# Layer 1: q and k turned by DMA, attention one group behind its pair group

## The chip, the cores and the metric

The kernel runs on one core of one Trainium2 chip. The metric is the device time of one execution in microseconds (us). The core has TensorE (matrix multiply, results to PSUM, eight banks of 128 partitions by 2 KB), VectorE, ScalarE, GpSimd, and SyncE, which issues most of the transfers; 16 DMA engines move the data.

## The reference

A decoder trunk of two layers over 256 tokens of width 2048, float32. Every layer is: RMSNorm, mixer, residual add, RMSNorm, SwiGLU FFN (hidden 5632), residual add; a last RMSNorm ends it. Layer 0 mixes with sliding-window attention beside an mLSTM. Layer 1, where the change lies, mixes with a forgetting attention of 16 heads of width 128:

```python
proj = xn @ w_in                         # (256, 2048) @ (2048, 3*2048 + 16)
q, k, v, f = split_cols(proj, FOX_SIZES)
log_f = jax.nn.log_sigmoid(f + b_f)
c = cumsum(log_f, axis=1)                # one bias per head and token
s = einsum('bhqd,bhkd->bhqk', q, k) * 128 ** -0.5
s = s + c[query] - c[key]                # causal: other scores are -inf
out = einsum('bhqk,bhkd->bhqd', softmax(s), v) @ w_out
```

## The kernel before

**Products.** Float32 operands are split into a high and a low part, and a product is three matmuls: high by high, high by low, low by high. A weight chunk is 256 rows by up to 512 columns (512 KB). `load_raw` (L111) loads it from SyncE's queue, `split_chunk` (L160) casts the high part on ScalarE (L163) and subtracts on VectorE (L164); six split chunks and four raw ones can be in flight. `gemm` (L177) is a plain product of one 512-column block, 12 matmuls of 512 columns per chunk (2 slices of k, 2 blocks of 128 tokens, 3 products).

**Pair groups.** `pair_group` (L487) makes two 512-column blocks at once, here q and k of four heads. It walks eight pairs of k slices in the order `QK_ORDER`; five are plain (24 matmuls), three are "mixed": a Strassen-like form of 21 matmuls, for which VectorE and ScalarE form sums and differences of the two weight chunks (L518 to L530) and split them. The second chunk of a mixed pair goes to a raw tile of the mixer's own pool (`od`, tag `raw`, two buffers). The plain sums take four PSUM banks of one pool and the products four of the other; `par` says which (`par` 0: plain sums in `pa`, products in `pm`). At the end the products are gathered in `c`, a tile of four 512-column rows (q of two token blocks, then k), and `fold` (L687) adds the plain sums, scaled by the norm.

**The mixer of layer 1** (from L1038) does this four times, for four heads each: a pair group; the values of the next group (`v_part`, a plain product in two `pm` banks), in parts that serve as filler; 16 turns of 128 by 128 blocks of q and k on TensorE (`transpose_many`, L297, matmuls with the identity at L301, evicted by VectorE at L302); and `attention` (L304). The last group's filler is the first part of the output product (`begin`), since no values are left.

**Attention** of four heads: scores in two halves (heads 0 and 2, then 1 and 3; L312, L319), scaled and biased on VectorE into `s` (L313, L320), which overlies `c`; maxima (L326); exponentials on ScalarE (L341); normalising on VectorE (L354). After a first `yield`, the probabilities are turned on TensorE (L363, L367). After a second, they meet the values (L371, L372), and the result is split into `mh` and `ml` (L382), the operand of the output product.

**Order.** The program is written once in Python; a scheduler with a timing model then fixes the order of each engine's queue. A higher place in the text means a higher priority; an instruction written later can be put ahead where the model finds it ready and the earlier one not. `tc.issue_after(x)` keeps what is written under it behind instruction `x`. On the chip, each queue runs in that order. `turn_scaled` (L251) and the FFN (L595 to L605) already turn tiles by DMA: a float32 tile is split into two planes of 16-bit halves (ScalarE), each plane is turned by one DMA transpose from SyncE's queue (`turn_planes`, L237), and the turned planes are joined again (ScalarE, L247 for the FFN).

Of the kernel before, what the change touches and what calls it, by code (L numbers as in the profile page):

```python
# [17 lines left out]
P = 128  # L18
# [6 lines left out]
CK = 2  # L25
# [35 lines left out]
def trunk(  # L61
# [90 lines left out]
        nc.sync.dma_start(bias_f, fox_b_f[0].partition_broadcast(P))  # L152

    latest = [None]

    def load_chunk(w, k0, c0, n):
        raw = ahead.pop(0) if ahead else load_raw(w, k0, c0, n)
# [19 lines left out]
    def gemm(acc, lhs, w, c0, n, k_from, k_to, k_all, skew=1):  # L177
        k0 = k_from
        while k0 < k_to:
            last = k_to == k_all and k0 + skew * CK >= k_all  # L180
            chunks = [load_chunk(w, kc, c0, n) for kc in range(k0, k_all if last else k0 + CK, CK)]
            order = [(i, t) for i in range(len(chunks) * CK) for t in range(NT)]
            if last:
                order.sort(key=lambda it: it[1])
            for i, t in order:
                k = k0 + i
                hi, lo = (c[:, i % CK, 0:n] for c in chunks[i // CK])
                ah, al = lhs(k)
# [4 lines left out]
                nc.tensor.matmul(o, al[:, ts], hi, start=False, stop=(k == k_all - 1))  # L193
            k0 += len(chunks) * CK

    def x_of(k):
# [104 lines left out]
            nc.tensor.transpose(pt[:, i, :], s_, ident)  # L301
        nc.vector.tensor_copy(dst, pt[:, 0:m, :])  # L302

    def attention(sp, q_of, k_of, v_of, dv, scale, bias0, bias1, k_tile, sinks=None, negc=None, s=None, ps=(pm, "pm")):  # L304
        if s is None:
            s = sp.tile([P, 4, 3 * P], F32, tag="s", name="s", bufs=2)
        for half in range(2):
            hs = slice(half, 4, 2)
            p0 = ps[0].tile([P, 2, P], F32, tag=ps[1], name="p0")
            for jj in range(2):  # L310
                j = 2 * jj + half
                nc.tensor.matmul(p0[:, jj, :], q_of(j, 0), k_of(j)[:, 0:P], start=True, stop=True)  # L312
            nc.vector.scalar_tensor_tensor(  # L313
                out=s[:, hs, 0:P], in0=p0, scalar=scale, in1=bias0[:, hs, :], op0=ALU.mult, op1=ALU.add
            )
            p1 = ps[0].tile([P, 2, S], F32, tag=ps[1], name="p1")
            for jj in range(2):
                j = 2 * jj + half
                nc.tensor.matmul(p1[:, jj, :], q_of(j, 1), k_of(j), start=True, stop=True)  # L319
            nc.vector.scalar_tensor_tensor(  # L320
                out=s[:, hs, P : 3 * P], in0=p1, scalar=scale, in1=bias1[:, hs, :], op0=ALU.mult, op1=ALU.add
            )
        parts = (slice(0, P), slice(P, 3 * P))
        mx = sm.tile([P, NT, 4], F32, tag="mx", name="mx")
        for b in range(NT):
            nc.vector.reduce_max(mx[:, b, :], s[:, :, parts[b]], axis=AX)  # L326
        neg = sm.tile([P, NT, 4], F32, tag="neg", name="neg")
        den = sm.tile([P, NT, 4], F32, tag="den", name="den")
        if sinks is not None:
# [7 lines left out]
            )  # L337
        for b in range(NT):
            for j in range(4):
                e = s[:, j, parts[b]]  # L340
                nc.scalar.activation(  # L341
                    e, e, AF.Exp, bias=neg[:, b, j : j + 1], accum_out=den[:, b, j : j + 1]
                )
        if sinks is not None:
# [5 lines left out]
        nc.vector.reciprocal(rec, den)  # L350
        for b in range(NT):
            for j in range(4):
                e = s[:, j, parts[b]]
# [4 lines left out]
        for half in range(2):  # L358
            pt = pm.tile([P, 2, S], F32, tag="pm", name="pp")
            for jj in range(2):  # L360
                j = 2 * half + jj
                for b in range(NT):
                    nc.tensor.transpose(pt[:, jj, b * P : (b + 1) * P], s[:, j, b * P : (b + 1) * P], ident)  # L363
            nc.scalar.copy(t0[:, 2 * half : 2 * half + 2, :], pt)
        pt = pm.tile([P, 4, P], F32, tag="pm", name="pp1")
        for j in range(4):
            nc.tensor.transpose(pt[:, j, :], s[:, j, 2 * P : 3 * P], ident)  # L367
        nc.vector.tensor_copy(t1, pt)

        def pv(po, j):  # L370
# [668 lines left out]
    with tc.tile_pool(name="od", bufs=1) as od:  # L1039
        def nat1(acc, n, name, bufs=1):  # L1040
            t_ = od.tile([P, NT, n], F32, tag=name, name=name, bufs=bufs)
            for t in range(NT):
                nc.scalar.mul(t_[:, t, :], acc[t][:, 0:n], r1[:, t : t + 1])
            return t_

        gemm(vacc0, x_of, wi1, c_v, NB, 12, KT, KT)
        vns = {0: nat1(vacc0, NB, "vn", bufs=2)}
        acc = tacc1
        gemm(acc, x_of, wi1, c_v + 14 * FD, VT + FOX_H, 8, KT, KT)
        fg = od.tile([P, NT, FOX_H], F32, name="fg")  # L1050
# [23 lines left out]
            j = mixed.index(pair)  # L1074
            return sx[0][:, j, :, :], sx[1][:, j, :, :]

        def v_part(i):
            vw = NB if i < 3 else VT
            acc = [bank(1, "vacc") for _ in range(NT)]

            def part(k0, k1):
                gemm(acc, x_of, wi1, c_v + i * NB, vw, k0, k1, KT)
                if k1 == KT:
                    vns[i] = nat1(acc, vw, "vn", bufs=2)

            return part
# [15 lines left out]
        for i in range(4):  # L1102
            qt = od.tile([P, 4, S], F32, tag="qt", name="qtf")
            kt = od.tile([P, 4, S], F32, tag="kt", name="ktf")
# [7 lines left out]
            if i == 3:  # L1112
                halves[:] = [halves[1], None]
            plain, c = pair_group(
                room, 0, x_of, sums_q, [(wi1, i * NB), (wi1, FOX_H * FD + i * NB)], QK_ORDER
            )
            fold(plain, c, (r1, r1))
            if i < 3:
                part = v_part(i + 1)
                fillers = [lambda k=k: part(k, k + 4) for k in (0, 4)] + [lambda: part(8, KT), lambda: None]  # L1120
            else:
                begun = [new_acc() for _ in range(2)]

                def begin(m, k0, k1):
                    return lambda: gemm(begun[m], m_of, w_out_odd[0], m * NB, NB, k0, k1, KT)

                def both(*some):
                    return lambda: [one() for one in some]

                fillers = [begin(0, 0, 4), begin(0, 4, 8), both(begin(0, 8, 12), begin(1, 0, 4)), begin(1, 4, 12)]  # L1130
            ps = (pa, "acc") if i < 3 else (pm, "pm")
            fillers.pop(0)()
            for m, dst in enumerate((qt, kt)):
                for g in range(0, 4, 2):
                    transpose_many(
                        dst[:, g : g + 2, :].rearrange("p g (t q) -> p (g t) q", q=P),
                        [c[:, 2 * m + t, (g + u) * FD : (g + u + 1) * FD] for u in range(2) for t in range(NT)],
                        ps,
                    )
            vn = vns[i]  # L1140

            def v_of(j, b, i=i, vn=vn):
# [4 lines left out]
            fillers.pop(0)()  # L1147
            for _ in attention(
                od,
                lambda j, b, qt=qt: qt[:, j, b * P : (b + 1) * P],  # L1150
                lambda j, kt=kt: kt[:, j, :],
                v_of,
                FD,
                FD**-0.5,
                cb0,
                cb1,
                4 * i,
                negc=negc[:, :, 4 * i : 4 * i + 4],
                s=c[:, :, 0 : 3 * P],
                ps=ps,  # L1160
            ):
                fillers.pop(0)()


    ov = out[0].rearrange("(t p) d -> p t d", p=P)
    fs = cp.tile([P, NT, 4], F32, name="fs")
# [27 lines left out]
    close_layer(1, w_out_odd[0], 3, "f1", begun=begun, finish=finish)  # L1194


_INS = [
# [46 lines left out]
```

## Time and profile before

| what | value |
|---|---|
| time, three runs | 2100.2, 2102.77, 2104.49 us; median 2102.77 |
| profiled execution | 2100.61 us, of which the span from first to last instruction is 2098.9 |
| TensorE busy | 2085.3 us, 99% of the span |
| VectorE, ScalarE busy | 1818.7 us (87%), 1325.4 us (63%) |
| DMA | 429.33 MB, mean 205 GB/s |
| mean granted TensorE clock | 0.999 |

A row of the stretches has its start and end, its length, then for each engine the busy time and the number of instructions, then the granted clock, the busy share of the DMA engines and GB/s. A row of a group has line, engine, operation, output and inputs, shapes and count; then the busy total, the mean ns of one; then the idle time of the engine before them and what ended it. A row of the chain has start, duration, engine, output, line and count. A row of the order in time has start, duration and the instruction, and in brackets the idle time before it. A row of the waits has who waited for whom, the total, the times and the longest. DMA issues have size and median us to landing.

### The profile page before, as it was taken

The page shows a single profiled execution, that of the slowest core. Times are in us where ns is not written, and L with a number is a line of the kernel's source. Part 1 is how long each engine was busy: PE and PEld are TensorE (multiplying, and loading weights), DVE is VectorE, ACT ScalarE, POOL GpSimd, SP SyncE. Part 2 cuts the span into 40 slices and gives each one's busy share as a digit, 9 for nine tenths or more (in the row PEclk, how much of TensorE's full clock was granted, in tenths as well). Part 3 has the DMA queues.
Part 4 walks back from the last instruction along what each step waited for, and adds up shares of the span by engine and source line. Part 5 has one row for each costly group of instructions (what it writes and reads, how often), then busy time and mean ns, then how long its engine had stood idle before and what let it go on. Part 6 is the DMA issues. An engine that isn't in the chain of part 4 may idle for free.

```text
span 2098.9 us, 26844 instructions
## 1 busy us (share of the span) xinstructions
PE 2085.3 (99%) x9582; PEld 1732.6 (83%) x9582; DVE 1818.7 (87%) x2402; ACT 1325.4 (63%) x1685; POOL 45.6 (2%) x70
## 2 busy tenths in 40 slices
PE   9999999999999999999999999999999999999998
PEld 7878888888888888888888888888888888888886
DVE  6689768998999999998898877679989999999985
ACT  7565568665577656667865555586755677556763
POOL 2100000000000000000000000000000000000000
PEclk9999999999999999999999999999999999999999
DMA  9446667766576657766775565577756676657763
GB/s 330 123 131 211 209 192 234 238 197 201 189 235 213 218 192 220 211 211 187 202 258 164 176 189 164 180 231 222 239 170 225 206 215 216 214 191 230 215 197 136
DMA packets 283318, 429.33 MB, mean 205 GB/s; under 512 B 80928, under 2 KB 89136, under 8 KB 283184
## 3 DMA queue, kind: packets, MB, share of 16 engines
q1 hardware_dynamic: 281424, 421.80, 64.8%
q0 software_dynamic: 1616, 5.78, 0.8%
q8 instruction: 75, 1.23, 0.2%
q14 instruction: 59, 0.48, 0.1%
q10 hardware_dynamic: 144, 0.03, 0.0%
HBM read 408.67 MB, written 2.11 MB: 196 GB/s over the span
## 4 chain that ended last, share of the span: by engine, by line
PE 92%; DVE 5%; issue 1%; DMA 1%; ACT 1%; POOLq 0%; POOL 0%; SPq 0%; DVEq 0%; ACTq 0%
PE acc L413 19%; PE acc L412 19%; PE acc L414 19%; PE acc L193 5%; PE acc L192 5%; PE acc L191 5%; PE prod L412 5%; PE prod L414 5%; PE prod L413 5%; DVE lo L164 2%; PE vacc L193 1%; PE vacc L192 1%; PE vacc L191 1%; DMA raw<-in_w_up_dram 1%; PE ptm L301 1%
## 5 line engine op out<-in xcount | busy, mean ns | idle before, releaser
L163 ACT CAST hi<-raw 128x1024 fp32r<-128x1024 f32 (+1 forms) x664 | 675.2, 1031 | 462.1 <-PE acc L414 223.3
L164 DVE TENSOR_TENSOR lo<-raw,hi 128x1024 fp32r<-128x1024 f32 (+1 forms) x664 | 785.8, 1198 | 137.0 <-ACT hi L163 135.0
L413 PE MATMUL acc<-lo,xh 128*128 128x512 f32 x1207 | 470.8, 390 | 0.4 <-DVE lo L164 0.4
L414 PE MATMUL acc<-hi,xl 128*128 128x512 f32 x1207 | 468.0, 390 | 0.0
L412 PE MATMUL acc<-hi,xh 128*128 128x512 f32 x1207 | 465.2, 390 | 1.0 <-DVE c L545 1.0
L412 PEld LDWEIGHTS acc<-hi,xh 128*128 128x128 f32 x1207 | 226.6, 188 | 49.1 <-DVE c L545 1.8
L413 PEld LDWEIGHTS acc<-lo,xh 128*128 128x128 f32 x1207 | 226.7, 188 | 47.5 <-DVE lo L164 0.7
L414 PEld LDWEIGHTS acc<-hi,xl 128*128 128x128 f32 x1207 | 226.7, 188 | 47.0
L413 PE MATMUL acc<-lo,mh 128*128 128x512 f32 x444 | 173.0, 390 | 0.0
L414 PE MATMUL acc<-hi,ml 128*128 128x512 f32 x444 | 171.5, 390 | 0.0
L412 PE MATMUL acc<-hi,mh 128*128 128x512 f32 x444 | 169.9, 390 | 0.0
L289 ACT CAST ht<-t 128x1024 fp32r<-128x1024 f32 x94 | 98.8, 1051 | 55.2 <-PE prod L414 48.7
L289 ACT CAST ht<-raw 128x1024 fp32r<-128x1024 f32 x94 | 98.6, 1049 | 44.6 <-PE acc L414 18.0
L191 PE MATMUL acc<-hi,mh 128*128 128x512 f32 x320 | 126.3, 396 | 0.0
L192 PE MATMUL acc<-lo,mh 128*128 128x512 f32 x320 | 125.0, 391 | 0.0
L193 PE MATMUL acc<-hi,ml 128*128 128x512 f32 x320 | 125.0, 393 | 0.0
L290 DVE TENSOR_TENSOR lt<-raw,ht 128x1024 fp32r<-128x1024 f32 x94 | 114.8, 1221 | 11.7 <-ACT ht L289 11.6
L289 ACT CAST hi<-raw 128x512 fp32r<-128x512 f32 (+1 forms) x115 | 72.3, 629 | 77.6 <-PE acc L414 60.8
L290 DVE TENSOR_TENSOR lt<-t,ht 128x1024 fp32r<-128x1024 f32 x94 | 114.6, 1219 | 5.5 <-ACT ht L289 5.5
L413 PEld LDWEIGHTS acc<-lo,mh 128*128 128x128 f32 x444 | 83.4, 188 | 17.3
L412 PEld LDWEIGHTS acc<-hi,mh 128*128 128x128 f32 x444 | 83.4, 188 | 17.3
L414 PEld LDWEIGHTS acc<-hi,ml 128*128 128x128 f32 x444 | 83.4, 188 | 17.1
(384 smaller groups left out, 3550.1 us busy)
## 6 DMA issues: line engine op xcount, KB each, us to landing
raw<-in_w_gate_dram SPq DMA_DIRECT2D x176, 512.0 KB, 4.6
raw<-in_w_up_dram SPq DMA_DIRECT2D x176, 512.0 KB, 4.7
raw<-in_w_down_dram SPq DMA_DIRECT2D x176, 512.0 KB, 4.8
raw<-in_w_in_odd_dram SPq DMA_DIRECT2D x88, 512.0 KB, 4.5
raw<-in_w_in_even_dram SPq DMA_DIRECT2D x64, 512.0 KB, 4.7
raw<-in_w_out_even_dram SPq DMA_DIRECT2D x32, 512.0 KB, 4.1
raw<-in_w_out_odd_dram SPq DMA_DIRECT2D x32, 512.0 KB, 4.9
raw<-in_w_in_odd_dram SPq DMA_DIRECT2D x8, 272.0 KB, 3.2
```

The costliest lines, as they stand in the source:

```text
L163: latest[0] = nc.scalar.copy(hi[:, :, 0:n], raw[:, :, 0:n])
L164: nc.vector.tensor_tensor(out=lo[:, :, 0:n], in0=raw[:, :, 0:n], in1=hi[:, :, 0:n].bitcast(F32), op=ALU.subtract)
L191: nc.tensor.matmul(o, ah[:, ts], hi, start=(k == 0), stop=False)
L192: nc.tensor.matmul(o, ah[:, ts], lo, start=False, stop=False)
L193: nc.tensor.matmul(o, al[:, ts], hi, start=False, stop=(k == k_all - 1))
L289: nc.scalar.copy(dst_h, src)
L290: nc.vector.tensor_tensor(out=dst_l, in0=src, in1=dst_h.bitcast(F32), op=ALU.subtract)
L301: nc.tensor.transpose(pt[:, i, :], s_, ident)
L412: nc.tensor.matmul(o, ah, hi, start=start, stop=False)
L413: nc.tensor.matmul(o, ah, lo, start=False, stop=False)
L414: nc.tensor.matmul(o, al, hi, start=False, stop=stop)
```

## The change

Pair groups of layer 1 run one ahead of the attention. Group 0 is only made; then, for i = 1 to 3, pair group i is made and group i-1 attended during the value product of group i; group 3 is attended at the end, with output products as filler. q and k of every group are turned by DMA, in the planes described above, in places that stand free at that time: the planes of q turn in `t0` or `t4`, those of k in small temporaries, and the heads go to `qt` and `kt` with two buffers each. The scores of groups 0 to 2 lie in the pool's two raw tiles, one per half, in place of `c`; for that `attention` takes `s` as two tiles, and its maxima are taken per half (four reduces in place of two) wherever it is called, layer 0 too. The first half's scores take `pa` banks, the second's `pm`. The values have one buffer and lie in `pa` banks; pair groups 1 to 3 have `par` 1. The special case of the last pair group's operand tiles (`halves[:] = [halves[1], None]`) goes.

```diff
+TURN_QK = (0, 1, 2, 3)
+SCORES_AT = -1
...
-    def attention(sp, ..., s=None, ps=(pm, "pm")):
+    def attention(sp, ..., s=None, ps=((pm, "pm"), (pm, "pm"))):
         if s is None:
-            s = sp.tile([P, 4, 3 * P], F32, tag="s", name="s", bufs=2)
+            whole = sp.tile([P, 4, 3 * P], F32, tag="s", name="s", bufs=2)
+            s = [whole[:, a:4:2, :] for a in range(2)]
...
         for b in range(NT):
-            nc.vector.reduce_max(mx[:, b, :], s[:, :, parts[b]], axis=AX)
+            for half in range(2):
+                nc.vector.reduce_max(mx[:, b, half:4:2], s[half][:, :, parts[b]], axis=AX)
...
-        vns = {0: nat1(vacc0, NB, "vn", bufs=2)}
+        vns = {0: nat1(vacc0, NB, "vn")}
...
+        def turn_heads(c, places):
+            cu = c.bitcast(U16).rearrange("p a (n b) -> p a n b", b=2)
+            heads, starts, joins = [], [], []
+            for m, turned in enumerate(places):
+                a = od.tile([P, 4, S], F32, tag=("qt", "kt")[m], name="heads", bufs=2)
+                au = a.rearrange("p g s -> p (g s)").bitcast(U16)
+                flat = au.rearrange("p (b n) -> p b n", b=2)
+                for b in range(2):
+                    nc.scalar.copy(flat[:, b, :].rearrange("p (t n) -> p t n", t=NT), cu[:, 2 * m : 2 * m + 2, :, b])
+                def start(flat=flat, turned=turned):
+                    with tc.issue_after(load[0].ins):
+                        turn_planes(turned, flat)
+                def join(au=au, turned=turned):
+                    cb = au.rearrange("p (n b) -> p n b", b=2)
+                    for b in range(2):
+                        nc.scalar.copy(
+                            cb[:, :, b].rearrange("p (g t q) -> p g t q", g=4, t=NT),
+                            turned[b].rearrange("p (t g) q -> p g t q", t=NT),
+                        )
...
+            return heads, starts + joins
...
         for i in range(4):
-            ... (pair group i with par 0, fold, values of i + 1 as filler,
-                 transpose_many of q and k, attention of i with s=c[:, :, 0 : 3 * P])
+            plain, c = pair_group(
+                room, min(i, 1), x_of, sums_q, [(wi1, i * NB), (wi1, FOX_H * FD + i * NB)], QK_ORDER, todo
+            )
+            fold(plain, c, (r1, r1))
+            if i == 0:
+                t0 = od.tile([P, 4, S], F32, tag="t0", name="turn0", bufs=1)
+                heads, steps = turn_heads(c, [place(t0.rearrange("p g s -> p (g s)")), small_places()])
+                todo = list(zip(TURN_QK, steps))
+                continue
+            t4 = room.t4()
+            new, steps = turn_heads(c, [place(t4.rearrange("p a n -> p (a n)")), small_places()])
+            spare = [od.tile([P, CK, NB], F32, tag="raw", name="s", bufs=2) ... for _ in range(2)]
+            gen = attend(i - 1, heads, spare, ((pa, "acc"), (pm, "pm")))
+            heads = new
+            w = NB if i < 3 else VT
+            vacc = [bank(0, "vacc") for _ in range(NT)]
+            if i == 3:
+                parts = [lambda a=a: values(a, a + 4) for a in range(0, 16, 4)]
+                parts += [lambda a=a: begin(0, a, a + 2) for a in range(0, 8, 2)]
+            else:
+                parts = [lambda a=a: values(a, a + 2) for a in range(0, 16, 2)]
+            for n, part in enumerate(parts):
+                if i == 3 and n == 4:
+                    begun[0] = new_acc()
+                if n == 0 and SCORES_AT < 0:
+                    next(gen)
+                part()
+                if n in (SCORES_AT, 4, 6):
+                    next(gen, None)
+                if n in (2, 3):
+                    run_next(steps)
+            vns[i] = nat1(vacc, w, "vn")
+            todo = list(enumerate(steps))
+        while steps:
+            with tc.issue_after(last_exp[0].ins):
+                run_next(steps)
+        begun[1] = new_acc()
+        gen = attend(3, heads, [c[:, a:4:2, 0 : 3 * P] for a in range(2)], ((pm, "pm"), (pm, "pm")))
+        begin(0, 8, 10)
+        with tc.issue_after(last_mm[0].ins):
+            next(gen)
+        begin(0, 10, 12)
+        begin(1, 0, 6)
+        next(gen)
+        begin(1, 6, 10)
+        next(gen, None)
+        begin(1, 10, 12)
```

`todo` hands steps to the next pair group: each is run at the named position of its walk, behind the cast of that position's chunk. `attend(i, ...)` is the former call of `attention` for group i, with the loads of its bias (`cb1`, `cb0`) ahead of it.

More of the change, by code (lines that the diff above doesn't have):

```diff
@@ L154, in trunk @@
     latest = [None]
+    last_mm = [None]
+    last_exp = [None]
     def load_chunk(w, k0, c0, n):
@@ L320, in attention @@
             nc.vector.scalar_tensor_tensor(
-                out=s[:, hs, P : 3 * P], in0=p1, scalar=scale, in1=bias1[:, hs, :], op0=ALU.mult, op1=ALU.add
+                out=s[half][:, :, P : 3 * P], in0=p1, scalar=scale, in1=bias1[:, hs, :], op0=ALU.mult, op1=ALU.add
             )
@@ L366, in attention @@
         for j in range(4):
-            nc.tensor.transpose(pt[:, j, :], s[:, j, 2 * P : 3 * P], ident)
+            nc.tensor.transpose(pt[:, j, :], s[j % 2][:, j // 2, 2 * P : 3 * P], ident)
         nc.vector.tensor_copy(t1, pt)
@@ L1075, in sums_q @@
             return sx[0][:, j, :, :], sx[1][:, j, :, :]
[L1077 to L1086, printed above, removed]
         pc = pm.tile([P, NB], F32, tag="pm", name="pcf")
@@ L1101, in trunk, with place, small_places, attend @@
         nc.gpsimd.dma_start(scratch, negct)
-        for i in range(4):
-            qt = od.tile([P, 4, S], F32, tag="qt", name="qtf")
-            kt = od.tile([P, 4, S], F32, tag="kt", name="ktf")
+        def turn_heads(c, places):
[17 more added lines that the diff above has]
+                        )
+                heads.append(a)
+                starts.append(start)
+                joins.append(join)
+            return heads, starts + joins
+        def place(tile_):
+            v = tile_.bitcast(U16)
+            return [v[:, b * 2 * NB : (b + 1) * 2 * NB].rearrange("p (i q) -> p i q", q=P) for b in range(2)]
+        def small_places():
+            return [od.tile([P, 8, P], U16, tag="tmp", name="turned", bufs=2) for _ in range(2)]
+        def attend(i, heads, s, ps):
+            qt, kt = heads
             cb1 = od.tile([P, 4, S], F32, tag="cb1", name="cb1", bufs=1)
@@ L1111, in trunk, with v_of @@
                 )
[L1112 to L1139, printed above, removed]
             vn = vns[i]
-            def v_of(j, b, i=i, vn=vn):
+            def v_of(j, b):
                 if i == 3 and j >= 2:
@@ L1158, in trunk, with begin, values @@
                 negc=negc[:, :, 4 * i : 4 * i + 4],
-                s=c[:, :, 0 : 3 * P],
+                s=s,
                 ps=ps,
-            ):
-                fillers.pop(0)()
+            )
+        def begin(m, k0, k1):
+            gemm(begun[m], m_of, w_out_odd[0], m * NB, NB, k0, k1, KT)
+        begun = {}
+        todo, heads = [], None
+        for i in range(4):
+            plain, c = pair_group(
+                room, min(i, 1), x_of, sums_q, [(wi1, i * NB), (wi1, FOX_H * FD + i * NB)], QK_ORDER, todo
+            )
+            fold(plain, c, (r1, r1))
+            flat_c = c.rearrange("p a n -> p (a n)")
+            if i == 0:
[5 more added lines that the diff above has]
+            new, steps = turn_heads(c, [place(t4.rearrange("p a n -> p (a n)")), small_places()])
+            spare = [
+                od.tile([P, CK, NB], F32, tag="raw", name="s", bufs=2)
+                .rearrange("p a n -> p (a n)")[:, 0 : 6 * P]
+                .rearrange("p (j n) -> p j n", j=2)
+                for _ in range(2)
+            ]
+            gen = attend(i - 1, heads, spare, ((pa, "acc"), (pm, "pm")))
+            heads = new
+            w = NB if i < 3 else VT
+            vacc = [bank(0, "vacc") for _ in range(NT)]
+            def values(k0, k1):
+                gemm(vacc, x_of, wi1, c_v + i * NB, w, k0, k1, KT)
+            if i == 3:
[15 more added lines that the diff above has]
+            todo = list(enumerate(steps))
@@ L1192, in finish @@
                 nc.sync.dma_start(ov[:, t, hs], h[:, t, hs])
-    close_layer(1, w_out_odd[0], 3, "f1", begun=begun, finish=finish)
+    close_layer(1, w_out_odd[0], 3, "f1", begun=[begun[0], begun[1]], finish=finish)
 _INS = [
```

25 lines of the change are left out of this document (12 added, 13 removed).

## The prediction

> **What bounds the kernel now.** I read the page's busy shares first, then busy time by stretches, then the chain of work that ended last. All times are microseconds (us).
>
> The page's head and its first engine line:
> ```profile
> span 2098.9 us, 26844 instructions
> ...
> PE 2085.3 (99%) x9582; PEld 1732.6 (83%) x9582; DVE 1818.7 (87%) x2402; ACT 1325.4 (63%) x1685; POOL 45.6 (2%) x70
> ```
> Stretches: the first two rows lie in the layer-1 mixer that the change rewrites (its four groups run from about 1075 to 1352) and hold one value pass, one attention group and one pair group each; the third lies in the first FFN.
> ```profile
> core 0: us, PE busy (x) PEld busy (x) DVE busy (x) ACT busy (x) POOL busy (x), PEclk, DMA share, GB/s
> 1106.00:1176.00 70.00, 70.00 (x333) 58.58 (x332) 56.65 (x75) 40.34 (x58) 1.77 (x3) 1.00 0.61 185
> 1176.00:1246.00 70.00, 70.00 (x344) 59.19 (x343) 54.39 (x75) 36.59 (x57) 3.54 (x3) 1.00 0.53 155
> ...
> 530.00:1040.00 510.00, 509.15 (x2268) 422.66 (x2267) 473.19 (x588) 333.75 (x375) 0.00 (x0) 1.00 0.69 209
> ```
> TensorE is busy for every microsecond of the two cycles, at the full granted clock. Busy is modelled, so I look at how far apart matmuls start: in the chain three 512-column matmuls take 0.68, 0.227 each, and a clump of turns for the heads takes 1.75 for 16, 0.109 each. The first row below is such a clump, q and k of one whole group.
> ```profile
> 1246.27 1.75 PE ptm L301 x16
> ...
> 1298.26 0.68 PE acc L412 x3
> ```
> So this stage is a stream of TensorE work without holes. Removing TensorE work there shortens the run one for one; removing work or waits from another engine is worth nothing; adding work elsewhere costs only what starves TensorE.
>
> **The change part by part.** *Turns leave TensorE.* The grouped view of 1040 to 1370 has the turns and their evictions:
> ```profile
> L163 ACT CAST hi<-raw 128x1024 fp32r<-128x1024 f32 x95 | 98.6, 1050 | 80.6 <-PE vacc L193 25.5 <-PE acc L414 13.4 <-PE acc L193 13.4
> ...
> L301 PE MATMUL ptm<-ident,c 128*128 128x128 f32 x64 | 8.3, 273 | 0.0
> ...
> L302 DVE COPY qtf<-ptm 128x512 f32<-128x512 f32 x8 | 5.2, 685 | 1.4 <-PE ptm L301 1.4
> ...
> L326 DVE TENSOR_REDUCE mx<-c 128x4 f32<-128x1024 f32 x4 | 4.9, 1214 | 0.0
> ...
> L326 DVE TENSOR_REDUCE mx<-c 128x4 f32<-128x512 f32 x4 | 2.7, 679 | 0.0
> ```
> All 64 go: 64 x 0.109 = 7.0 off the path. The 273 ns of the row is start to modelled end and overlaps the next matmul; the spacing in the chain is what the path pays. The Trainium skill's page "TensorE: Matmul & The Clock Gate", Part 4: PE-mode transpose, gives about 275 ns for a turn inside a kernel. The trace agrees on the duration (273) but not as a price: paid one after another, 64 would be 17.6, and the sum, with the small losses below, 2086.5. The sum goes by 7.0. The other matmuls (scores, values, probabilities) keep their count. The evictions leave VectorE, 8 for q in the row and as many for k: 16 x 0.685 = 11, all under TensorE, worth nothing by itself.
>
> *Turns arrive on ScalarE, SyncE and DMA.* Each group splits q and k into two 16-bit planes each (4 copies), turns them (4 DMA transposes) and joins them (4 copies). The FFN has the same operations at the same shapes; its grouped view (530 to 1040) and the DMA issues:
> ```profile
> L247 ACT COPY c<-turned 128x1024 uint16<-128x1024 uint16 x20 | 25.8, 1352 | 0.0
> ...
> L599 ACT COPY c<-c 128x1024 uint16<-128x1024 uint16 x16 | 15.9, 1041 | 0.0
> ...
> raw<-in_w_in_odd_dram SPq DMA_DIRECT2D x88, 512.0 KB, 4.5
> ...
> turned<-c SPq DMA_TRANSPOSE x52, 4.0
> ```
> ScalarE gets 4 x 1.04 + 4 x 1.35 = 9.6 per group, 38 in all. In the 70 us rows it was busy 40.3 and 36.6, so it goes to about 50 of 68. Its casts wait mostly for TensorE to free buffers (L163's releasers), that is, they run ahead to the limit. Cost on the path: nothing on average. If that lead were gone, a block of 4.2 of splits or 5.4 of joins in front of a cast would come through whole, at most 38 over the four groups; from below nothing, since a copy shortens no TensorE work. The FFN is nearest: it turns planes the same way with VectorE busy 473 of 510 and TensorE lost 0.85 in 510. I take 0 for this.
>
> DMA: four transposes of 4.0 to landing per group queue on SyncE among the weight loads. SyncE waits today for buffers, not for bandwidth:
> ```profile
> SPq L113 <- DVE lo L164: 960.9, 462, 11.6
> ...
> SPq L242 <- ACT c L599: 47.8, 15, 5.6
> ```
> A transpose that waits for its split holds the loads queued behind it (5.6 at worst in the FFN's row). Weights already split cover that: the pools hold six chunks of 12 matmuls, 6 x 12 x 0.227 = 16. I take 0; from above, the excess of a late transpose over 16, which would need a hold three times that row's worst.
>
> *One group ahead.* Group i-1 is now attended during the value pass of group i, after pair group i, so its q and k have a whole pair group to be turned in (183 matmuls x 0.227 = 41.5). That hides the turns' latency: splits 4.2, transposes 16 if one lands after another, joins 5.4, together 26. Pair groups 0 and 1 now follow each other directly, with plain sums and products in alternate PSUM pools, as FFN groups do.
>
> *What can become late.* From pair group 1 on, the plain sums sit in the pool (pm) that the attention uses for half of its scores, its turned probabilities and its outputs. Before, the next pair group started in the other pool, and the attention could finish behind it. Here is group 1's attention today (chain, and VectorE in order of time): its scores, the start of the next pair group, the last split of its output.
> ```profile
> 1185.26 0.43 PE p L319 x2
> ...
> 1198.58 0.23 PE acc L412
> ...
> 1215.00 0.69 DVE L290 TENSOR_TENSOR ml<-po,mh 128x512 fp32r<-128x512 f32 x1 [0.18 <-ACT mh L289]
> ```
> That is 30.4 from 1185.3 to 1215.7, and the next pair group ran from 1198.6 on in its shadow. The last group, with less around it, took 22.6:
> ```profile
> 1324.66 0.61 PE L312 MATMUL p<-ktf,qtf 128*128 128x128 f32 x4
> ...
> 1346.61 0.69 DVE L290 TENSOR_TENSOR ml<-po,mh 128x512 fp32r<-128x512 f32 x1 [0.19 <-ACT mh L289]
> ```
> After the change the cover is the value pass, 96 x 0.227 = 21.8, the attention's own TensorE work (16 matmuls of 256 columns at 0.43 / 2 and, with the turns of probabilities, 28 of 128 columns at 0.109: 6.5), and the first 12 matmuls of the next pair group, which need only two of the four banks: 2.7. Together 31.0. The chain there: 22.6 to 30.4 as seen, plus 4.2 of splits if they queue ahead of the exponentials, plus up to two joins, 2.7. Less what no longer mixes in: group 1's attention shared VectorE with preparation of the next mixed pair, which now cannot start while the scores hold those raw tiles; some 4 us, my estimate from the 7.8 by which this chain is longer than the last group's. So shortfall per place: below zero (no loss) at best, 30.4 + 4.2 + 2.7 - 31.0 = 6.3 at worst. Nearest is the row of group 1 with its 4 taken off and the splits put on, 30.6: about level. I take 0.4 for each of three places (behind pair groups 1, 2, 3), 1.2.
>
> The raw tiles: the next group's second weight matrix cannot load until the scores are turned, some 20 into the value pass. It is needed about 28 + 11 = 39 in, less 4.5 for the load and 5 for preparation: some 10 of slack, cost 0; if the turned probabilities came over 10 late, the excess.
>
> *The end of the mixer.* Scores of group 3 now have behind them begun output products of k 10 to 12 for the first half and 0 to 12 for the second: 14 k, 84 x 0.227 = 19.1, and 6.5 of their own, 25.6, against a chain of 22.6 there today. It holds, by 3. One value buffer: written after the last reader; 0.
>
> *Layer 0.* The reduces are halved for all eight groups. From the two L326 rows, 512 more elements cost 0.535, so each instruction has a fixed 0.144, and two more make 0.29 on VectorE per group. In the mixer that lies under TensorE. For the four groups of layer 0 the bounds are 1.2 less and 1.2 more (all of 4 x 0.29 comes through, or half scores that can be reduced earlier save as much); I take 0.1, near nothing, because VectorE has 13% of idle time over the run.
>
> **Sum.** -7.0 + 1.2 + 0.1 = -5.7. The profiled execution took 2100.61 (span 2098.9 and 1.7 around it), 2.16 under the median of the three runs, 2102.77. 2100.61 - 5.7 = 2094.9; on the median's scale 2097.1.
>
> **The rivals.** *A: most of the gain is given back.* Two of the three places lose 2 to 2.5, because order on each queue is fixed ahead and an exponential or a join sits behind a cast: -7.0 + 4.5 + 0.5 = -2, 2100.8. For it: splits, exponentials and joins all fall into the 28 after a pair group, beside 8 casts, so ScalarE's mean of 50 in 68 hides a stretch with no spare time. Against it: casts are 16 ahead, and neither cycle has a hole today.
>
> *B: slower, through the pm banks.* The worst chain, 37.3, meets a cover of 31: 6.3 at each of three places, 18.9 - 7.0 = +11.9, 2114.7. The mechanism decides from a loss of 7.0 in all, or 2.3 per place; it is measurably slower from 3.7 per place. For it: 30.4 today already nearly equals the cover. Against it: today nothing hurries that chain, since work of the next pair group lies ready, and where less lay around it, in the last group, it took 22.6.
>
> *C: the whole gain, and no loss.* 7.0: 2095.8. It is an end of the forecast's own range.
>
> *D: the turns are hidden already.* Then nothing changes: 2102.8. Against it: the clumps stand in the chain with nothing beside them on TensorE.
>
> *E: the page's price of a turn.* Its rule, each turn paid whole, gives with the 273 ns row 17.5, less the 1.3 of losses, 2086.6; the 1.75 for 16 speaks against it.
>
> **How the numbers follow.** About 0.2%, 4.2, is what a measurement can tell from no change; the runs shown spread by 4.3. Forecast with C: 0.65, own range 2094.5 to 2098.6. A: 0.18. B: 0.12. D: 0.03. E: 0.02. Faster by over 0.2% (under 2098.6): forecast, C and E with a little of A, 0.68. Within 0.2%: 0.20, from A, D and a mild B. Slower: 0.12. The range starts at 2094.5 (no loss and 1 of spread) and reaches to 2103.5, over A and D; what it leaves out is B, E and the spread's tails.
>
> **What would show it right or wrong.** Right: no L301 row on c in the mixer; 32 splits and joins on ScalarE and 16 more transposes on SyncE; TensorE still full in each stretch, and the mixer's end some 6 earlier. A shows as waits of TensorE for score or output evictions at the start of a pair group, a few tenths to 2 each. B shows as waits there above 3.7 for an ml or mh split. Wrong altogether: TensorE waiting for weights behind a transpose, or holes before pair group 1, where I see none.

## The result and the profile after

The changed kernel takes 2096.06 us (median of 8 runs, 2093.9 to 2096.61). The kernel before, run beside it, takes 2101.69 (8 runs, 2100.2 to 2104.49). The ratio is 0.997, with a 95% interval of 0.9959 to 0.9981: faster by 5.6, against a forecast of 5.7 less. The profiled execution took 2093.9; its span follows, from the page of after:

```profile
span 2092.2 us, 26777 instructions
...
PE 2078.2 (99%) x9518; PEld 1725.2 (82%) x9518; DVE 1809.4 (86%) x2402; ACT 1358.4 (65%) x1717; POOL 42.0 (2%) x70
```
Against before, TensorE has 64 instructions and 7.1 us less, VectorE 9.3 less, ScalarE 33 more. So the turns left TensorE, and their copies are on ScalarE.

To see where the time went I cut each span in three: to the first matmul of the layer-1 mixer (the column sums of its decays), the mixer (to the last GpSimd step of the norm behind it), and the rest. The mixer is one stretch in the view of busy time by stretches. Before:

```profile
core 0: us, PE busy (x) PEld busy (x) DVE busy (x) ACT busy (x) POOL busy (x), PEclk, DMA share, GB/s
1073.90:1404.50 330.60, 330.60 (x1597) 278.48 (x1597) 252.42 (x340) 197.15 (x292) 12.19 (x13) 1.00 0.63 190
```
After, the whole mixer, then its first three cycles and its end:

```profile
1074.10:1398.70 324.60, 323.90 (x1533) 271.56 (x1533) 242.31 (x332) 229.40 (x324) 8.53 (x13) 1.00 0.71 207
...
1075.00:1141.60 66.60, 66.60 (x295) 55.15 (x296) 58.79 (x68) 49.04 (x55) 3.17 (x4) 1.00 0.74 228
1141.60:1211.90 70.30, 70.30 (x325) 58.37 (x325) 55.46 (x74) 48.86 (x68) 1.84 (x3) 1.00 0.76 204
1211.90:1281.80 69.90, 69.90 (x325) 58.41 (x324) 53.03 (x75) 47.34 (x67) 1.76 (x3) 1.00 0.60 173
1281.80:1317.40 35.60, 34.91 (x215) 31.17 (x214) 22.30 (x36) 25.14 (x42) 1.76 (x3) 1.00 0.82 245
```
Length minus TensorE's busy time is its idle time. The mixer went from 330.6 to 324.6, 6.0 shorter. It had no idle TensorE before; after, it is full through all three cycles, in which ScalarE stands at 47 to 49 of 66 to 70 as forecast, and idle for 0.69 at the end. So TensorE's busy time fell by 6.7 and the end took 0.7 back. Layer 0 and the first FFN became 0.2 longer (1073.9 to 1074.1; layer 0 has the maxima by halves), and the rest 0.9 shorter (694.4 to 693.5), in code that the change doesn't touch.

The groups of instructions in after show what was added:

```profile
L1107 ACT COPY heads<-c 128x1024 uint16<-128x1024 uint16 x16 | 15.7, 1042 | 0.8 <-DVE c L698 0.8
...
L1116 ACT COPY heads<-turned 128x1024 uint16<-128x1024 uint16 x8 | 10.3, 1348 | 0.0
L1116 ACT COPY heads<-t 128x1024 uint16<-128x1024 uint16 x6 | 7.7, 1354 | 0.0
...
L1116 ACT COPY heads<-turn 128x1024 uint16<-128x1024 uint16 x2 | 2.6, 1354 | 0.0
```
That is 16 splits and 16 joins, 36.3 us, at the durations of the FFN's rows, and no join ever waited (idle 0.0): its transposes had landed before its place in the queue came up. In the view of waits TensorE has one new entry in the mixer. In order of time it lies ahead of group 3's scores (1317.25), so the output that is missing is that of group 2, whose attention runs behind pair group 3:

```profile
PE acc L195 <- ACT mh L293: 0.7, 1, 0.7
```
```profile
1311.44 0.50 PE L195 MATMUL acc<-hi,mh 128*128 128x512 f32 x1 [0.69 <-ACT mh L293]
...
1317.25 0.61 PE L317 MATMUL p<-heads 128*128 128x128 f32 x4
```
The chain of work names the way there:

```profile
1297.96 1.71 ACT heads L1116 x2
...
1300.39 2.12 ACT heads L1116 x2
...
1303.87 0.95 ACT hi L167
1304.85 1.24 DVE lo L168
1306.10 3.65 DMA raw<-in_w_out_odd_dram
1309.86 1.05 ACT hi L167
1310.91 0.49 ACT mh L293
```
Read it from the bottom. TensorE waits for the split of the attention's output (mh), which stands on ScalarE behind a cast (hi, 1309.86), which waits for a weight load. That load started late, as it needs the raw tile that the cast at 1303.87 and its lo part on VectorE release, and that cast stood behind the four joins of group 3. So the joins make no hole where they run; the load that is issued later for them does, 10 us on.

### The profile page after: what moved, and what is told of

It is laid out like the page before. It is cut to its first block, busy times and chain, and to the rows that moved or that the text cites. A ratio compares the mean times of both kernels' runs of the same rounds, so it can differ in the third digit from the quotient of the medians.

```text
span 2092.2 us, 26777 instructions
## 1 busy us (share of the span) xinstructions
PE 2078.2 (99%) x9518; PEld 1725.2 (82%) x9518; DVE 1809.4 (86%) x2402; ACT 1358.4 (65%) x1717; POOL 42.0 (2%) x70
## 4 chain that ended last, share of the span: by engine, by line
PE 94%; DVE 3%; issue 1%; DMA 1%; ACT 1%; POOLq 0%; POOL 0%; SPq 0%; ACTq 0%; DVEq 0%
PE acc L418 20%; PE acc L419 20%; PE acc L420 20%; PE prod L418 5%; PE prod L420 5%; PE prod L419 5%; PE acc L195 5%; PE acc L197 5%; PE acc L196 5%; PE vacc L195 1%; PE vacc L196 1%; PE vacc L197 1%; DVE lo L168 1%; PE p L324 0%; DMA raw<-in_w_in_even_dram 0%
## 5 line engine op out<-in xcount | busy, mean ns | idle before, releaser
L418 PE MATMUL acc<-hi,xh 128*128 128x512 f32 x1204 | 463.2, 390 | 0.8 <-DVE c L551 0.8
L418 PEld LDWEIGHTS acc<-hi,xh 128*128 128x128 f32 x1204 | 225.9, 188 | 49.2 <-DVE c L551 1.6
L418 PE MATMUL acc<-hi,mh 128*128 128x512 f32 x444 | 169.6, 389 | 0.0
L294 DVE TENSOR_TENSOR lt<-raw,ht 128x1024 fp32r<-128x1024 f32 x94 | 114.4, 1217 | 10.8 <-ACT ht L293 10.8
L294 DVE TENSOR_TENSOR lt<-t,ht 128x1024 fp32r<-128x1024 f32 x94 | 114.3, 1216 | 5.0 <-ACT ht L293 4.9
L293 ACT CAST hi<-raw 128x512 fp32r<-128x512 f32 x112 | 69.3, 619 | 73.5 <-PE acc L420 53.9
L418 PEld LDWEIGHTS acc<-hi,mh 128*128 128x128 f32 x444 | 83.3, 188 | 17.3
```

What stands on the lines that cost most here:

```text
L293: nc.scalar.copy(dst_h, src)
L294: nc.vector.tensor_tensor(out=dst_l, in0=src, in1=dst_h.bitcast(F32), op=ALU.subtract)
L418: nc.tensor.matmul(o, ah, hi, start=start, stop=False)
```

## The experiments

The theory: TensorE is the only bound of this stage, a turn is worth its spacing of 0.109, and all that the change adds elsewhere lies under TensorE. The rivals: the gain comes from the new order and not from the turns; or the copies, the transposes or the pm banks are near a limit. Mixer and rest are cut as above.

**All turns back on TensorE, in the new order.**
```
                 a = od.tile([P, 4, S], F32, tag=("qt", "kt")[m], name="heads", bufs=2)
+                def turn(m=m, a=a):
+                    for g in range(0, 4, 2):
+                        transpose_many(a[:, g : g + 2, :] ..., [c[:, 2 * m + t, ...] ...], (pa, "acc"))
+                heads.append(a)
+                starts.append(turn)
+                continue
                 ... (splits, DMA transposes and joins, which are no longer reached)
```


> The changed kernel with its 64 turns of q and k back on TensorE (evicted by VectorE), in the new order: one group ahead, scores in the raw tiles, one value buffer. Theory (the gain is the 64 turns, at 0.109 us each, that left TensorE; the order by itself is worth nothing): 7.0 us come back, so about 2096.1 + 7.0 = 2103.1, or 2102.4 if the new hole of 0.7 at the mixer's end closes with the joins gone; ratio to the kernel before 1.000 to 1.001. Rival (the gain comes from running the pair groups ahead, which gives the attention more cover): it stays at about 2096, ratio 0.997.

Measured: 2103.16 (11 runs), ratio 1.0007 (0.9997 to 1.0016). The mixer's stretch:

```profile
1075.70:1407.10 331.40, 330.79 (x1597) 278.37 (x1597) 251.37 (x348) 196.50 (x292) 8.75 (x13) 1.00 0.62 190
```
331.4 against 324.6 in after, 6.8 more, with 6.9 more of TensorE's busy time. With the turns back on TensorE the whole gain is gone, so the order by itself is worth nothing that these runs can show.

**The reverse: turns by DMA, in the old order.** Group i is still attended behind its own pair group.
```
 # against the kernel before, behind the fold of a group
-  transpose_many(dst ..., [c[:, ...]], ps)        # q and k
+  nc.scalar.copy(flat[:, b, :] ..., cu[:, 2*m : 2*m+2, :, b]); turn_planes(places[m], flat)
 ... (first piece of filler)
+  nc.scalar.copy(cb[:, :, b] ..., places[m][b] ...)    # joins
```


> The kernel before, in its old order (attention of group i right behind pair group i), with only the turns of q and k changed to DMA planes. Theory: TensorE work falls by the same 7.0 us, but splits 4.2, transposes 4 to 16 and joins 5.4 now stand in the chain from pair group to scores, 14 to 26, against 21.8 of value products beside them; the scores come some 10 us later than today, and as the score and value banks are shared with the next pair group, TensorE waits: 0 to 10 per group, so 2095 to 2135, most likely some 2110, slower than before. Rival (the order does not matter, only the turns do): 2102 - 7 = 2095, as fast as the changed kernel.

Measured: 2110.07 (4 runs), ratio 1.0042 (1.0028 to 1.0056). The largest wait of TensorE, which ends at 1261.75, and three stretches of 2 us around that point:

```profile
PE p L312 <- ACT ktf L1147: 7.2, 1, 7.2
```
```profile
1260.00:1262.00 2.00, 0.25 (x1) 0.25 (x2) 0.05 (x1) 2.00 (x3) 0.00 (x0) 0.50 1.03 380
1262.00:1264.00 2.00, 2.00 (x7) 1.77 (x8) 1.43 (x3) 2.00 (x3) 0.00 (x0) 0.50 1.06 408
...
1266.00:1268.00 2.00, 2.00 (x11) 1.65 (x10) 2.00 (x4) 0.00 (x0) 0.00 (x0) 1.00 0.86 252
```
The scores wait 7.2 for the join of k. Over the mixer TensorE is idle for 10.6, and behind this hole the granted clock stands at 0.50 before it is 1.00 again. So the turns by DMA need the order, and the order is worth nothing without them: the change's two halves give together what neither gives alone.

**Half of the turns back: q's.** The edit is that of the first experiment, with its last three lines under `if m == 0`.

> The other half dose: the turns of q back on TensorE, those of k on DMA. Theory (32 turns cost 3.5; the 2.1 more that the first half dose lost in the mixer were holes of its own order, a join that waited for its transpose ahead of the exponentials, and weights that loaded late behind it): mixer 324.6 + 3.5 = 328.1 plus what holes this order has, which its own waits of TensorE must account for to within a few tenths; time 2099 to 2102. Rival (a half dose costs as much as the full one, whatever waits): mixer 331 without holes that explain it, 2103.

Measured: 2098.27 (10 runs), ratio 0.9981 (0.9971 to 0.999).

```profile
1075.70:1402.70 327.00, 327.00 (x1565) 275.07 (x1566) 248.71 (x340) 214.50 (x308) 8.78 (x14) 1.00 0.67 199
```
TensorE has no hole here, nor in before: 32 turns fewer took the mixer from 330.6 to 327.0, 3.6. The price per turn is even, 0.11.

**Half of the turns back: k's.** The same, with `if m == 1`.

> The changed kernel with the turns of k back on TensorE and those of q left on DMA: half the dose. Theory: 32 turns at 0.109 come back, 3.5 us, so 2099.6 (2098.9 if the hole at the end closes); ratio 0.9986. Rival (the gain is all or nothing, because it hangs on a wait that vanishes): 2096 or 2103.

Measured: 2102.43 (11 runs), ratio 1.0003 (0.9994 to 1.0012): a miss, 2099.6 had been expected. The same number of turns as in the run above costs 4 more. ScalarE in order of time shows a likely reason for part of it:

```profile
1160.64 2.58 ACT L1129 COPY heads<-t 128x1024 uint16<-128x1024 uint16 x2 [1.03 <-DMA t<-heads]
...
1180.87 0.62 ACT L293 CAST hi<-raw 128x512 fp32r<-128x512 f32 x1 [6.64 <-DMA raw<-in_w_in_odd_dram]
```
Without k's steps the join of q comes up sooner than its transpose has landed, and holds the exponentials behind it by 1.03. The raw tiles that hold the scores come free after them, and a later cast waits 6.64 for its load; that the first causes the second is read from the order, not tried by itself. The mixer is 330.2, with 2.27 of idle TensorE at three places. Two of them, 0.6 and 0.5, lie around that late cast; the third, 1.2 at 1308.20, is a wait for VectorE's eviction of the turns. 327.0 and 2.27 are 329.3, and 0.9 stays unexplained. The profiled execution, the slowest of the eleven, also lost 4.6 against after ahead of the mixer, in the same code (last section). With the run above, the price of a turn stands; what differs is which half goes back.

**ScalarE: every split and join twice.**
```
-  for b in range(2):
+  for b in (0, 1, 0, 1):      # at L1106 and L1115
```


> The changed kernel with every split and every join of the planes made twice: 9.6 us more on ScalarE per group, 38 in all, nothing on TensorE; ScalarE of the stretch from 1142 to 1212 goes from 48.9 to about 58.5 of 70. Theory (ScalarE is under cover): 0 to 1 us in the three cycles; at the mixer's end, where a cast already delayed the output split, up to 5.4 more of joins stand ahead of it, so 2096 to 2101.5, ratio 0.997 to 0.9995. Rival (ScalarE has no spare time in the 28 us behind a pair group, rival A of the prediction): every cycle loses several us, at least 10 in all, 2106 or more.

Measured: 2115.47 (5 runs), ratio 1.0062 (1.0049 to 1.0074). The theory missed, and the rival "no spare time" held. The stretches around the first hole:

```profile
1160.00:1170.00 10.00, 10.00 (x46) 8.24 (x45) 4.31 (x7) 9.97 (x18) 2.64 (x3) 1.00 0.92 255
1170.00:1180.00 10.00, 5.07 (x20) 3.24 (x18) 6.22 (x13) 10.00 (x17) 0.00 (x0) 0.68 0.75 204
1180.00:1190.00 10.00, 8.62 (x29) 6.80 (x30) 6.43 (x10) 9.88 (x13) 0.00 (x0) 0.64 0.46 161
```
ScalarE is busy for 29.9 of these 30 while its mean over the mixer is 262.4 of 342.3. TensorE is idle for 4.9 in the second row, in three waits of 1.35, 1.54 and 1.85, and the mean granted clock is 0.64 in the third. The mixer takes 17.7 more than in after: 10.1 more of idle time, and the rest is TensorE's own work at a lower clock. A second dose of these copies costs 17.7 where the first cost 0.7.

**DMA: every transpose twice.**
```
         turn_planes(turned, flat)
+        turn_planes(turned, flat)
```


> The changed kernel with every DMA transpose of q and k issued twice, into the same place: 16 more transposes, 5.2 us more of SyncE's queue and some 8 us more of DMA landing per group, nothing on the compute engines; the joins come that much later. Theory (the DMA side is under cover: weights are split 16 us ahead and the heads are wanted a pair group later): 0 to 1 us, 2096 to 2097. Rival (the weight loads behind the transposes are the tight place, as a cast at the mixer's end waited 2.2 us for its load): 1 to 4 us per group, 2100 to 2112.

Measured: 2109.34 (5 runs), ratio 1.0037 (1.0024 to 1.0049). Here too the theory missed and the rival (loads behind the transposes are tight) held. The largest wait of TensorE in the mixer, and the chain ahead of it:

```profile
PE po L377 <- ACT t L370: 6.1, 2, 5.1
```
```profile
1163.43 1.24 SPq L246
...
1164.72 4.16 SPq L246
...
1168.97 4.79 DMA raw<-in_w_in_odd_dram
...
1173.84 1.04 ACT hi L167
1174.88 0.49 ACT t L370
```
SPq is SyncE's queue; L246 issues the transposes. They hold the queue for 5.4, the load behind them lands 4.8 later, the cast at the head of ScalarE's queue waits for it, and the attention's copy of turned probabilities (t) waits behind that cast, though its own data were there. Earlier in the same queue another cast had waited 3.31 for its load, and a pair of joins 0.85 for its second transpose. A late load reaches TensorE through what stands behind its cast.

**Less cover: the scores behind four pieces of the value pass.**
```
-SCORES_AT = -1
+SCORES_AT = 3
```


> The changed kernel with the scores of groups 0 to 2 issued after the fourth part of the value product in place of ahead of the first: 48 matmuls, 10.9 us later, nothing else changed. Theory (the attention must be done when the next pair group wants its pm banks; in the changed kernel the cover of 31 us is used up to a few us): cover falls to 20, and TensorE waits 2 to 6 us behind each of pair groups 1 and 2, and again at the end: 2100 to 2112. Rival (there is slack enough, as the latency is mostly queueing that nothing hurries): 2096 to 2098.

Measured: 2108.09 (6 runs), ratio 1.0031 (1.002 to 1.0042), in the theory's range, but not for its reason.

```profile
PE po L377 <- ACT t L370: 4.4, 1, 4.4
PE pp L369 <- DVE s L360: 3.2, 2, 2.2
```
The long ones, 2.2 and 4.4, lie behind pair group 3, where the four pieces are the whole value pass; behind pair group 1 it is 0.9, and behind pair group 2 no wait is listed. TensorE runs out of work and waits for the attention's own steps: the normalised scores (s) and the copy of the turned probabilities (t). So an attention needs TensorE work beside it. That a pm bank is what runs short, as the theory and rival B have it, this run doesn't show.

**The hole at the end: earlier filler, or a later join.** One run brings 12 begun matmuls forward, ahead of the last scores; the other moves one pair of joins behind the first begun products.
```
 # e4_tail_filler
+begin(1, 0, 2)
 begin(0, 8, 10)
 ...
-begin(1, 0, 6)
+begin(1, 2, 6)
 # e12_last_join_later
-while steps:
-    with tc.issue_after(last_exp[0].ins):
-        run_next(steps)
+with tc.issue_after(last_exp[0].ins):
+    run_next(steps)
 ...
 begin(0, 8, 10)
+run_next(steps)
```


> The changed kernel with one chunk of the second output product (k 0 to 2, 12 matmuls, 2.7 us) moved ahead of the first product of k 8 to 10, the one that waits for the output split of group 2. Theory (the one new hole of the mixer, 0.7 us, is that split standing behind a cast that waited for its load): the hole closes, 2096.1 - 0.7 = 2095.4, and the attention of group 3 keeps 23 us of cover against 22.6; ratio 0.9965. Rival (the hole is a late load, so it moves with whatever comes next): no change, 2096.1, or up to 2 slower if group 3 now lacks cover.

> The changed kernel with the join of k of the last group issued after the cast of the next output weights, in place of right behind the join of q: ScalarE's queue there differs by the order of three entries. Theory (the hole of 0.7 at the mixer's end is a chain that starts with 5.1 us of joins in front of a cast: cast, subtraction, raw tile free, load of 3.7, next cast, output split): that cast comes 2.6 earlier, the load with it, and the hole closes: mixer 323.9 in place of 324.6, no wait of TensorE in it, time 2095.4. Rival (the load is late for the transposes in SyncE's queue, not for the joins): the hole stays at 0.7 to 1.4, 2096 to 2096.5.

Earlier filler: 2096.49 (9 runs), ratio 0.9974 (0.9964 to 0.9984), and idle TensorE in the mixer goes up from 0.69 to 1.78. TensorE waits at the same place, for 1.4, and ScalarE for the same load (2.20 in after):

```profile
PE acc L195 <- ACT mh L293: 1.4, 1, 1.4
```
```profile
1311.92 1.04 ACT L167 CAST hi<-raw 128x1024 fp32r<-128x1024 f32 x1 [2.22 <-DMA raw<-in_w_out_odd_dram]
```
The other 0.4 is a wait behind pair group 1, `PE acc L418 <- DVE ml L294`, which the next section takes up.

Later join: 2095.57 (5 runs), ratio 0.9966 (0.9952 to 0.9979), and no hole:

```profile
1076.00:1399.50 323.50, 323.50 (x1533) 271.63 (x1533) 241.41 (x332) 229.61 (x324) 8.71 (x13) 1.00 0.69 207
```
```profile
1303.28 1.06 ACT L167 CAST hi<-raw 128x1024 fp32r<-128x1024 f32 x1
1304.23 2.57 ACT L1116 COPY heads<-turned 128x1024 uint16<-128x1024 uint16 x2
1306.66 2.94 ACT L167 CAST hi<-raw 128x1024 fp32r<-128x1024 f32 x3
1310.20 1.05 ACT L167 CAST hi<-raw 128x1024 fp32r<-128x1024 f32 x1 [0.61 <-DVE lo L168]
```
In this stretch no cast waits for a load any more. That the filler fails and the join's place helps shows the late load as the cause. The mixer is 1.1 shorter than in after. This is the best version run; by the medians it leads after by 0.5, less than these runs can tell apart, so that lead rests on the trace alone.

**k's joins on VectorE.**
```
-  nc.scalar.copy(
+  (nc.vector.tensor_copy if m else nc.scalar.copy)(
```


> The changed kernel with the joins of k (2 copies of 1.35 us per group) moved from ScalarE to VectorE, which lost 2.7 us of evictions per group. Theory after the run with doubled copies (ScalarE has no spare time behind a pair group, and its queue order delays the output split at the end): ScalarE loses 2.7 per group, the hole of 0.7 at the end closes or shrinks, 2095 to 2096; if a 16-bit strided copy is slow on VectorE (some 2 us or more each), 2097 to 2100. Rival (ScalarE under cover): no change, 2096.

Measured: 2099.49 (11 runs), ratio 0.9988 (0.998 to 0.9997).

```profile
L1116 DVE COPY heads<-turned 128x1024 uint16<-128x1024 uint16 x8 | 5.6, 760 | 9.5 <-DMA turned<-heads 9.5
```
The copy is shorter there, 0.76 against 1.35. But at its place in VectorE's order the transpose has not landed, and VectorE stands 9.5 in all. TensorE's idle time in the mixer is 2.6. The time fell into the expected branch of 2097 to 2100, for another reason than the copy's price.

## Why the prediction was right

The sign, the size and the main mechanism held: 5.6 less, from 64 turns off a stage that TensorE fills. Some of the smaller terms were right for other reasons than those given.

- *64 x 0.109 = 7.0.* Right, and shown by three pairs of kernels. Putting all back adds 6.9 of TensorE, and among the mixers without a hole (before, q's turns back, the later join) the steps are 330.6 to 327.0 to 323.5, 3.6 and 3.5 for 32 turns each. Rival E, each turn paid whole, would have asked 17.5. The Trainium skill's page "VectorE: DVE Perf Modes", Rules for kernel authors, says to turn 128x128 on TensorE where PSUM will do and by DMA otherwise, and its section The three transpose paths lists a turn as shorter on TensorE. The trace agrees that turning takes less there: 16 turns took 1.75, and each of the four transposes of a group 2.8 to 5.2 to landing (medians by tile, after). But turning on TensorE as the rule asks gave 2103.16 against 2096.06, since here TensorE's time is the bound and the DMA's is not.
- *ScalarE and DMA at 0.* Right for this dose: no idle TensorE in three cycles. The reasons given were too easy, though. That casts run ahead and that split weights cover 16 promised a reserve, and doubling the copies cost 17.7 in the mixer, doubling the transposes 13.0. The mean of ScalarE, 47 to 49 of 66 to 70, hides stretches of 10 in which it never rests:

```profile
1224.00:1234.00 10.00, 10.00 (x52) 8.38 (x51) 6.31 (x13) 10.00 (x13) 0.37 (x1) 1.00 0.83 270
```
- *0.4 at each of three places.* The three lost 0.1 to 0.2, 0 and 0.7, near the 1.2 in sum but not place by place, and both sides of the comparison were counted too short. Behind pair group 1, the first score starts at 1141.43, and a weight load of the next pair group (PEld, TensorE's weight load) waits until 1175.02 for the bank of the attention's output (po), which comes free once the low part, ml, is taken from it:

```profile
1141.43 0.61 PE L317 MATMUL p<-heads 128*128 128x128 f32 x4
```
```profile
1175.02 0.19 PEld L418 LDWEIGHTS acc<-hi,xh 128*128 128x128 f32 x1 [0.39 <-DVE ml L294]
```
  So the chain took 33.6, not 30.6. The matmul of that load is the 23rd of its pair group, which starts at 1169.91, and not the 13th: at a spacing of 0.227 it was due at 1174.90, so the cover was 33.5, not 31.0, and TensorE lost 0.1 to 0.2. Behind pair group 2 the first score and the two last splits are these:

```profile
1211.69 0.61 PE L317 MATMUL p<-heads 128*128 128x128 f32 x4
```
```profile
1242.59 1.28 DVE L294 TENSOR_TENSOR ml<-po,mh 128x512 fp32r<-128x512 f32 x2
```
  The first of the two ends at 1243.27, 31.6 after the score, and the 23rd matmul of the pair group, which starts at 1240.11, is due at 1245.1, so nothing was lost. Chain and cover came out about level, as forecast. Rival B's mechanism, a pair group that waits for a pm bank, is there, at a few tenths where it needed 2.3 per place; the 0.4 of the earlier filler is the same wait.
- *The third of these places, behind pair group 3,* gave 0.69, and by rival A's mechanism: a step of the attention stood behind a cast. No pair group follows there; the output products need group 2's output, and the four joins of group 3 had made a load late. I had costed joins as time on ScalarE, and not what the casts behind them release. The term for the end of the mixer, "holds by 3", is about group 3's scores, and held: TensorE has no hole behind them.
- *Layer 0, +0.1.* The span up to the mixer grew by 0.2; that is as small as forecast and within what two executions differ by.
- *Sum.* Forecast -5.7, or 2097.1; measured -5.6 and 2096.06, as the median before of eight runs is 1.1 under that of three. By the traces -6.0 in the mixer, +0.2 before it and -0.9 behind it make -6.7 for that pair of executions; the medians give -5.6. Agreement with the forecast to 0.1 is luck, as executions of one kernel differ by more. Rival A, 5 given back, did not come: 0.7 was, at one place.

## What to carry to other kernels

Price work that leaves a full engine by the spacing of its instructions, and look at the stage, not at the whole run, to see that the engine is full. "Hidden" is a statement about one dose: before adding more, look for the stretches where the engine that hides it is at 10 of 10, and for loads whose buffers its queue releases. Where work is placed between casts on an in-order queue, its cost can show up later, as a late load; moving it behind the cast that frees the buffer helped here, and bringing cover forward did not.

## What the runs showed of the hardware

**A long hole costs more than its length.** Behind the wait of 7.2 in the old order the granted clock is 0.50 in two stretches of 2 us and 1.00 again in that from 1266 on. Against the 323.5 of a mixer without a hole, the doubled copies have 10.8 of idle TensorE and take 18.8 longer, the doubled transposes 11.0 and 14.1. After the hole of 0.7 the mixer stays at 1.00. The Trainium skill's page "TensorE: Matmul & The Clock Gate", Why this matters for your kernels, warns of idle gaps over about 3 us between bursts, with a halved clock after one. The rows behind the wait of 7.2 agree. The doubled copies don't fit that length: their clock is down to 0.50 when only the first of the three waits, 1.35, is over.

```profile
1174.00:1175.00 1.00, 1.00 (x7) 1.00 (x6) 0.20 (x1) 1.00 (x2) 0.00 (x0) 0.50 0.01 4
```

**The clock also falls without such a hole, in some executions.** The same program text in layer 0, first in after and then in the run with k's turns on TensorE:

```profile
140.00:150.00 10.00, 9.93 (x63) 7.61 (x62) 7.03 (x22) 5.02 (x15) 0.11 (x1) 1.00 0.00 0
```
```profile
140.00:150.00 10.00, 9.92 (x59) 7.39 (x58) 7.64 (x24) 4.44 (x13) 0.11 (x1) 0.83 0.00 0
...
150.00:160.00 10.00, 10.00 (x38) 8.04 (x37) 8.48 (x14) 8.19 (x11) 0.00 (x0) 0.82 0.18 54
```
TensorE is idle for under 0.1 in both, and for about 0.5 in the 10 us ahead, yet one loses 0.17 of 10 and 0.18 of the next 10, some 3.5 us. In finer stretches its clock is at 0.50 from 147 to 152. The runs sort by the clock: of the kernel before, run beside the first experiment, those at a mean clock of 0.999 take 2101.29 (mean of 6), those at 0.997 2103.52 (mean of 4). That is over half of the spread of 4 between runs, and a reason to compare mixers rather than single spans here. What triggers it stays open.
